# Half of an output product moved into the neighbourhood attention, experts in overlapping pairs, weights laid out in one piece, and value products with odd and even keys abreast

## The chip, the cores and the metric

The kernel runs on one core of one Trainium2 chip, in one launch. Times are device microseconds. The inputs are rearranged on the host before the launch (a function `layout`), which is not timed. All matrices are float32; most products are made of three matmuls on numbers split into a high and a low half.

## The reference, cut to what matters

Two blocks run after each other on 512 tokens of 1024 numbers, each with two layers. A layer of the first block is an attention mixer, a cross attention to a memory, and a mixture of experts in which every expert takes its 64 best tokens. A layer of the second block projects the normed and modulated tokens into four groups of 256 columns (a Fourier mix, neighbourhood attention, a spatial gating and differential attention), joins them in one output product, and adds a feed-forward part. In layer 0 of this block 256 context tokens are carried along.

```python
def expert_choice_moe(h, w_router, w_gate, w_up, w_down):
    ...
    x_in = jax.vmap(lambda hb, ib: hb[ib])(h, idx)
    a = jnp.einsum('becd,edf->becf', x_in, w_gate)
    u = jnp.einsum('becd,edf->becf', x_in, w_up)
    y = jnp.einsum('becf,efd->becd', jax.nn.silu(a) * u, w_down)
    y = y * gate[..., None].astype(y.dtype)
    return jax.vmap(lambda ib, yb: jnp.zeros((S, D), yb.dtype).at[ib.reshape(-1)].add(yb.reshape(-1, D)))(idx, y)

def diff_attend(q1, q2, k1, k2, v, lam):
    scale = DIFF_QK_DIM ** -0.5
    s1 = jnp.einsum('bqhd,bkhd->bhqk', q1, k1).astype(jnp.float32) * scale
    s2 = jnp.einsum('bqhd,bkhd->bhqk', q2, k2).astype(jnp.float32) * scale
    p = jax.nn.softmax(s1, axis=-1) - lam * jax.nn.softmax(s2, axis=-1)
    return jnp.einsum('bhqk,bkhd->bqhd', p.astype(v.dtype), v)

def second_block(x, c, ctx, ...):
    ...
        y = jnp.concatenate([y_a, y_b, y_c, y_d], axis=-1) @ w_out[l]
    ...
        x = x + g1 * y
```

## The kernel before, in words

Tokens lie transposed: a tile `x` holds 128 of the 1024 numbers of all 512 tokens, and eight such tiles the whole state; `cx` are the same for the context. Tiles come from pools with a fixed number of buffers per name (the tables `MIX`, `EXP`, `DIF` and so on; those that begin with `P_` are of PSUM). Each engine works through its own queue in order. A scheduler fixes these orders when the kernel is built, from the order in which the code is written and from modelled times.

A weight comes as a raw tile `wr` from SyncE's DMA queue (L288), is split by ScalarE (L334) into `wh` and by VectorE (L335) into the rest `wl`; `mm3` (L347) then issues three matmuls for each product, at L353, L354 and L356. Activations are split in the same way by `split` (L358).

The experts (`experts`, L872) go in four groups of four. A group gathers its tokens with one-hot matmuls (L888) into `xin`. Then two pairs of experts follow. For each expert of a pair eight steps multiply `xin` with the gate and the up weights (L930; their two results of 64 rows stand in the two halves of a PSUM tile), ScalarE scales the result into `au`, PE transposes it (L936), ScalarE and VectorE make the gated `gg` of it (L938, L939). When both experts of the pair have their `gg`, the second product with the down weights follows (L948, the pair's two experts abreast), is scaled and split into `yy` (L365, L366), and is spread back to the tokens (L956). Weights (`we`) are 1 MB each, two for each of gate, up and down of an expert; their pool has 14 buffers in layer 0 and 12 in layer 1 (`NWE`). On the device a load takes 2 KB in one piece, four pieces for each partition.

In block 2 the stage `nat` (`na`, L1187) goes through units of one head and 128 queries: scores (L1209, L1210), softmax, transposes (L458), and products with the values (L492). The stage `dif` (`diff`, L1256) does so for the differential attention: `stacks` (L1244) copies 32-row pieces of queries and keys by DMA (L1252) into `w`, two score tiles `pD` of up to 768 keys follow (L1292), each with a maximum (L1295) and an exponent (L1296), a combination of both (L1302), transposes (L458), and six value products into one half of a PSUM tile (L492), which ScalarE copies out (L1319). At the end of a half of the heads, `finish` norms and splits the result.

The output product is written as a generator: eight column chunks `c`, in each a sum over eight row chunks `es`, a step being one `mm3`. `fill` (L476) takes steps of it and puts them behind PE's newest instruction. Before, `es` 0 to 5 (48 steps) are filled into `dif`, two steps per unit, and what is left of them, and `es` 6 and 7, follow in the stage `out`. The halves that it multiplies are `YX` and `YC`, made by `parts` (L1505); for the Fourier and gating results this is done at the start of `dif`, in `begin`.

Of the kernel before, what the change touches and what calls it, by code (L numbers as in the profile page):

```python
# [17 lines left out]
D = 1024  # L18
# [121 lines left out]
def layout(a):  # L140
# [18 lines left out]
    for n in ("ln_ffn", "sgu_ln_g_2", "sgu_ln_b_2", "sgu_b_2", "diff_lq1_2", "diff_lk1_2", "diff_lq2_2",  # L159
              "diff_lk2_2", "w_gate", "w_up", "w_down", "ada_w_2"):  # L160
        o[n] = a[n]
    for l in range(2):
# [23 lines left out]
        o[f"w2_out{l}"] = chunks(a["w_out_2"][l][:768], 2)  # L186
        o[f"w2_last{l}"] = chunks(a["w_out_2"][l][768:], 8)
# [12 lines left out]
NWE = (14, 12)  # L200
FIN = 0
NAP = 0
FILL = (2, 0, 0)
# [4 lines left out]
NAB = 7  # L208
# [10 lines left out]
HEADS = {"h": 18, **NORMS}  # L219
MIX = {"f": 4, "e": 3, "pt": 4, "sqm": 3, "lat": 6, "kg": 4, "qk": 12, "kr": 2, "vg": 2, "vm": 1, "wk": 2,  # L220
       "rope1": 1, "rope2": 1, "perm": 1, "wrt": 1}
# [15 lines left out]
P_WIN = {"pS": 4, "pT": 2, "pO": 2}  # L237
# [11 lines left out]
class Kernel:  # L249
# [622 lines left out]
    def experts(k, l, routed):  # L872
        nc = k.nc
        slots, slot, (aH, aL), T = routed
        for g in range(4):
            oh = []
            for t in range(4):
                o = k.t("oh", (128, 4, 64), F32R)
                nc.vector.tensor_tensor(o, slots, slot[:, t, 4 * g:4 * g + 4].unsqueeze(2).to_broadcast([128, 4, 64]),
                                        op=OP.is_equal)  # L880
                oh.append(o.rearrange("p e s -> p (e s)"))
            xin = [k.t("xin", (128, NK, 128)) for _ in range(2)]
            for c in range(NK + 1):
                p = k.ps("mm")
                for t in range(4):
                    for j in range(2):
                        w = T[t][j][:, c * 128:c * 128 + 128] if c < NK else (aH, aL)[j][:, t, :]
                        nc.tensor.matmul(p[:w.shape[1], :256], w, oh[t], start=(t == 0 and j == 0), stop=(t == 3 and j == 1))  # L888
                if c < NK:
                    gain = k.gain(("ln_ffn", l), c)  # L890
                    nc.vector.tensor_scalar(xin[0][:, c], p[:, :128], gain, None, op0=OP.mult)
                    nc.scalar.activation(xin[1][:, c], p[:, 128:256], AF.Copy, scale=gain)
                else:
                    ga = k.t("ga", (17, 256))
                    nc.vector.tensor_copy(ga, p[:17, :256])
            gates, roots, ohT = [], [], []
            for pr in range(2):
                p = k.ps("T")
                nc.tensor.transpose(p[:, :17], ga[:, pr * 128:pr * 128 + 128], k.ident[:17, :17])
                gt = k.t("s1", (128, 1))  # L900
                for h in range(2):
                    a = slice(64 * h, 64 * h + 64)
                    e = 4 * g + 2 * pr + h
                    nc.vector.tensor_copy(gt[a], p[a, e:e + 1])
                    r = k.t("s1", (128, 1))
                    for b in (slice(0, 64), slice(64, 128)):
                        nc.vector.tensor_copy(r[b], p[a, 16:17])
                    roots.append(r)
                gates.append(gt)
                p = k.ps("T")  # L910
                for t in range(4):
                    nc.tensor.transpose(p[:, t * 128:(t + 1) * 128],
                                        oh[t][:, pr * 128:pr * 128 + 128].bitcast(F32), k.ident)
                o = k.t("ohT", dt=F32R)
                nc.scalar.activation(o, p, AF.Copy)
                ohT.append(o)
            for pr in range(2):
                G = []
                for h in range(2):
                    e = 4 * g + 2 * pr + h  # L920
                    s = slice(h * 64, h * 64 + 64)
                    W = {}
                    for n in ("w_gate", "w_up"):
                        for kh in range(2):
                            W[n, kh] = k.load("we", k.i[n][l, e, kh * 512:kh * 512 + 512].rearrange(
                                "(c p) f -> p c f", p=128), (128, 4, 512))
                    p = k.ps("mm")
                    for c in range(NK):
                        for a, n in ((0, "w_gate"), (64, "w_up")):
                            nc.tensor.matmul(p[a:a + 64], xin[pr][:, c, s], W[n, c // 4][:, c % 4],  # L930
                                             start=(c == 0), stop=(c == NK - 1))
                    au = k.t("au")
                    nc.scalar.activation(au, p, AF.Copy, scale=roots[2 * pr + h])
                    p = k.ps("T", (128, 4, 128))
                    for t in range(4):
                        nc.tensor.transpose(p[:, t, :], au[:, t * 128:(t + 1) * 128], k.ident)  # L936
                    gg = k.t("gg", (128, 4, 64))
                    nc.scalar.activation(gg, p[:, :, 0:64], AF.Silu)  # L938
                    nc.vector.tensor_mul(gg, gg, p[:, :, 64:128])  # L939
                    G.append(gg)  # L940
                WD = [[k.load("we", k.i["w_down"][l, 4 * g + 2 * pr + h, :, half * 512:half * 512 + 512].rearrange(
                    "(c p) f -> p c f", p=128), (128, 4, 512)) for h in range(2)] for half in range(2)]
                yH, yL = k.t("yy", (128, D), F32R), k.t("yy", (128, D), F32R)
                for half in range(2):
                    p = k.ps("mm")
                    for t in range(4):
                        for h in range(2):
                            nc.tensor.matmul(p[64 * h:64 * h + 64], G[h][:, t, :], WD[half][h][:, t],  # L948
                                             start=(t == 0), stop=(t == 3))
                    s = slice(half * 512, half * 512 + 512)  # L950
                    k.split(p, yH[:, s], yL[:, s], scale=gates[pr])
# [547 lines left out]
    def groups(k, l, mod, gains, last):  # L1499

        nc = k.nc
        with k.scope(f"proj{l}", PROJ):
# [38 lines left out]
            with k.scope(f"pg{l}", P_DIF, PSUM), k.scope(f"dif{l}", DIF):  # L1541
# [37 lines left out]
                for _ in adds:  # L1579
                    pass  # L1580
# [147 lines left out]
```

## Time and profile before

| | us |
|---|---|
| median of three runs | 3131.39 (3127.49 to 3134.98) |
| the profiled execution | 3128.51 |
| its span in the trace | 3126.7 |
| PE busy | 2971.6 |
| VectorE busy | 1581.2 |
| ScalarE busy | 1205.4 |
| GpSimd busy | 280.7 |

The span is what the trace covers of the profiled execution. PE's time counts each stretch in which at least one matmul is under way. The mean granted clock of PE is 0.97 of its full 2.4 GHz.

### The profile page before, as it was taken

How to read it: one execution, taken by the hardware profiler on the slowest of the kernel's cores; microseconds unless marked ns; L12 is line 12 of the kernel's file. 1: busy time of each engine (PE TensorE's matmuls, PEld its weight loads, DVE VectorE, ACT ScalarE, POOL GpSimd, SP SyncE). 2: the span in 40 equal slices, each digit the busy share in tenths (PEclk: the TensorE clock that was granted, in tenths of full speed). 3: DMA queues.
4: the chain of work that ended last, by engine and by line, in shares of the span. 5: the costliest groups of instructions: out<-in, count | busy, mean ns of one | idle time of the engine just before them, and what ended most of it. 6: DMA issues, size and time to landing. Idle time of an engine off the chain costs nothing.

```text
span 3126.7 us, 42254 instructions
## 1 busy us (share of the span) xinstructions
PE 2971.6 (95%) x16816; PEld 2241.4 (72%) x16816; DVE 1581.2 (51%) x3071; ACT 1205.4 (39%) x2356; POOL 280.7 (9%) x281
## 2 busy tenths in 40 slices
PE   8999979998999988999998899999999998999998
PEld 5677764444666864444887778888888787878887
DVE  5666652224576644234537666334344547654444
ACT  4646431113565532113426554222222336542332
POOL 2111120001102101001300011000000100010000
PEclk9999989999999998999999899999999998999999
DMA  5423249994433228996222311111111222222221
GB/s 183 135 95 122 95 180 332 358 370 172 161 109 115 82 78 316 367 370 242 62 74 70 90 41 55 68 55 68 68 54 54 97 96 71 65 81 95 94 98 64
DMA packets 168756, 422.34 MB, mean 135 GB/s; under 512 B 12144, under 2 KB 21616, under 8 KB 152816
## 3 DMA queue, kind: packets, MB, share of 16 engines
q1 hardware_dynamic: 167536, 416.76, 37.9%
q0 software_dynamic: 1024, 2.89, 0.4%
q8 instruction: 133, 2.18, 0.3%
q14 instruction: 63, 0.52, 0.0%
HBM read 405.18 MB, written 2.10 MB: 130 GB/s over the span
## 4 chain that ended last, share of the span: by engine, by line
PE 89%; DVE 4%; ACT 3%; issue 1%; DMA 1%; POOL 0%; SPq 0%; POOLq 0%; ACTq 0%; DVEq 0%
PE pmm L354 12%; PE pmm L353 12%; PE pmm L356 12%; PE pmm L930 8%; PE pS L353 5%; PE pS L356 4%; PE pS L354 4%; PE pmm L948 4%; PE pT L458 4%; PE pO L704 3%; PE pmm L888 2%; PE pA L998 2%; PE pmm L956 2%; PE pT L492 2%; PE pT L394 1%
## 5 line engine op out<-in xcount | busy, mean ns | idle before, releaser
L334 ACT ACTIVATE wh<-wr 128x1024 fp32r<-128x1024 f32 (+1 forms) x195 | 202.3, 1038 | 533.7 <-PE pmm L354 364.9
L335 DVE TENSOR_TENSOR wl<-wr,wh 128x1024 fp32r<-128x1024 f32 (+1 forms) x195 | 242.0, 1244 | 279.4 <-ACT wh L334 279.0
L930 PE MATMUL pmm<-we,xin 128*64 128x512 f32 x1024 | 238.1, 596 | 0.0
L353 PE MATMUL pS<-h,wh 128*128 128x512 f32 (+1 forms) x480 | 190.0, 400 | 12.5 <-ACT wh L334 10.2
L1616 DVE SCALAR_TENSOR_TENSOR x<-pmm,ada,x 128x512 f32<-128x512 f32 (+1 forms) x136 | 95.5, 717 | 206.4 <-PE pmm L356 206.3
L354 PE MATMUL pmm<-h,wh 128*128 128x512 f32 (+1 forms) x480 | 186.1, 389 | 2.7 <-DVE h L1036 2.6
L354 PE MATMUL pS<-h,wh 128*128 128x512 f32 (+1 forms) x480 | 185.2, 386 | 3.3 <-DVE h L366 3.3
L356 PE MATMUL pS<-h,wl 128*128 128x512 f32 (+1 forms) x480 | 185.2, 390 | 1.9 <-DVE wl L335 1.9
L356 PE MATMUL pmm<-h,wl 128*128 128x512 f32 (+1 forms) x480 | 184.0, 385 | 0.0
L353 PE MATMUL pmm<-h,wh 128*128 128x512 f32 (+1 forms) x480 | 182.9, 390 | 0.9 <-ACT h L1031 0.9
L334 ACT ACTIVATE vh<-wr 128x1024 fp32r<-128x1024 f32 x68 | 71.8, 1060 | 272.9 <-PE pmm L354 237.3
L930 PEld LDWEIGHTS pmm<-we,xin 128*64 128x64 f32 x1024 | 72.8, 137 | 136.8 <-issue 128.8
L379 POOL TENSOR_TENSOR sq<-sq,sq 128x512 f32<-128x512 f32 (+1 forms) x49 | 61.0, 1245 | 1174.7 <-ACT sq L371 1137.6
L948 PE MATMUL pmm<-we,gg 128*64 128x512 f32 x512 | 143.1, 605 | 15.1 <-DVE gg L939 15.1
L460 ACT ACTIVATE pt<-pT 128x512 f32<-128x512 f32 (+1 forms) x200 | 109.6, 554 | 118.9 <-PE pT L458 118.4
L335 DVE TENSOR_TENSOR vl<-wr,vh 128x1024 fp32r<-128x1024 f32 x68 | 83.7, 1233 | 114.0 <-ACT vh L334 114.0
L353 PE MATMUL pmm<-hid,vh 128*128 128x512 f32 (+1 forms) x400 | 139.3, 348 | 0.0
L439 DVE TENSOR_REDUCE s<-pS 128x1 f32<-128x512 f32 (+1 forms) x200 | 124.2, 622 | 27.8 <-PE pS L356 22.0
L354 PE MATMUL pmm<-hid,wh 128*128 128x512 f32 (+1 forms) x400 | 133.9, 350 | 0.0
L354 PE MATMUL pmm<-hid,vh 128*128 128x512 f32 (+1 forms) x400 | 133.8, 347 | 0.0
L353 PE MATMUL pmm<-hid,wh 128*128 128x512 f32 (+1 forms) x400 | 131.3, 349 | 0.0
L446 ACT ACTIVATE e<-pS,s,rt 128x512 f32<-128x512 f32 (+1 forms) x160 | 117.4, 734 | 17.6 <-DVE s L441 17.2
(443 smaller groups left out, 7179.0 us busy)
## 6 DMA issues: line engine op xcount, KB each, us to landing
we<-in_w_gate_dram SPq DMA_DIRECT2D x64, 1024.0 KB, 11.1
we<-in_w_up_dram SPq DMA_DIRECT2D x64, 1024.0 KB, 10.6
we<-in_w_down_dram SPq DMA_DIRECT2D x64, 1024.0 KB, 13.5
wr<-in_w_ff_dram SPq DMA_DIRECT2D x64, 1024.0 KB, 4.8
wra<-in_ada_w_dram SPq DMA_DIRECT2D x96, 512.0 KB, 4.2
wr<-in_w_in_dram SPq DMA_DIRECT2D x27, 1024.0 KB, 4.8
wr<-in_w_o_dram SPq DMA_DIRECT2D x8, 1024.0 KB, 4.8
wr<-in_w_mkv_dram SPq DMA_DIRECT2D x8, 1024.0 KB, 4.9
```

The lines of the kernel that those rows point to most:

```text
L334: k.nc.scalar.activation(H[:, :m], raw[:, a:a + m], AF.Copy)
L335: k.nc.vector.tensor_sub(L[:, :m], raw[:, a:a + m], H[:, :m].bitcast(F32))
L353: mm(p, wH, xH, start=(first and j == 0), stop=False)
L354: mm(p, wH, xL, start=False, stop=False)
L356: mm(p, wL, xH, start=False, stop=(end and j == n - 1))
L439: nc.vector.reduce_max(m, s, axis=AX, negate=True)
L446: nc.scalar.activation(e, s, AF.Exp, bias=m, scale=1.0 if scale is None else scale, accum_out=z)
L458: k.nc.tensor.transpose(p[:, t - a, :], src[:, t * 128:(t + 1) * 128], k.ident)
L460: k.nc.scalar.activation(dst[:, a:b], p[:, :b - a, :], AF.Copy)
L930: nc.tensor.matmul(p[a:a + 64], xin[pr][:, c, s], W[n, c // 4][:, c % 4], start=(c == 0), stop=(c == NK - 1))
L948: nc.tensor.matmul(p[64 * h:64 * h + 64], G[h][:, t, :], WD[half][h][:, t], start=(t == 0), stop=(t == 3))
L1616: nc.vector.scalar_tensor_tensor(x, p, mod[:, 40 + o, j:j + 1], x, op0=OP.mult, op1=OP.add)
```

## The change

In the experts, `gather` holds what was at the head of a group, `opened` the first products of a pair up to `gg`, and `closed` its second product and the spreading. `closed` of a pair is written behind `opened` of the next. The gate, up and down weights, and those of `ada`, are laid out so that a partition's share of a load is one piece (8 KB, and 4 KB for `ada`). Pools get other sizes, and the weights' pool of the mixer another place. In `nat` the units go head by head, each head's operands are made when its turn comes, and 32 steps of the output product (part 0, `es` 0, 1, 4, 5) are spread over the units by a due count. The parts that these need are made at the start of `nat`, with the subtraction on GpSimd. In `dif` part 1 (`es` 2, 3; 16 steps) is filled, one step per unit, and `out` has part 2. `halved` takes the place of `weigh` for the differential values: even keys go to the lower half of the PSUM tile, odd keys to the upper, ScalarE copies one half and VectorE adds the other.

```diff
-NWE = (14, 12)
+NWE = (13, 11)
-FILL = (2, 0, 0)
+FILL = (1, 0, 0)
...
-ROUTED = {"ht": 8, "ap": 2, "slots": 1, "oh": 4, "ga": 1, "xin": 2}
+ROUTED = {"ht": 8, "ap": 2, "slots": 1, "oh": 4, "ga": 1, "xin": 3}
 MOE = {"e16": 5, "m8": 2, "raw": 3}
-EXP = {"au": 2, "gg": 3, "yy": 3, "ohT": 2}
+EXP = {"au": 2, "gg": 4, "yy": 3, "ohT": 3}
...
-P_WIN = {"pS": 4, "pT": 2, "pO": 2}
+P_WIN = {"pS": 3, "pT": 2, "pO": 1, "pD": 1}
...
+    for n in ("w_gate", "w_up"):
+        o[n] = np.ascontiguousarray(a[n].reshape(2, 16, 2, 4, 128, 512).transpose(0, 1, 2, 4, 3, 5))
+    o["w_down"] = np.ascontiguousarray(a["w_down"].reshape(2, 16, 4, 128, 2, 512).transpose(0, 1, 4, 3, 2, 5))
...
+    def halved(k, e, v, nt, o, tag, work=None):
+
+        pt, p = k.t(tag, (128, nt, 128)), None
+        k.transposed(e, nt, pt, work=work)
+        p = k.ps("T", (128, 128))
+        for t in range(nt):
+            k.nc.tensor.matmul(p[64 * (t % 2):64 * (t % 2) + 64], v(t), pt[:, t, :], start=(t < 2), stop=(t >= nt - 2))
+        k.nc.scalar.activation(o, p[64:], AF.Copy)
+        k.nc.vector.tensor_add(o, o, p[:64])
...
     def experts(k, l, routed):
...
+        left = None
         for g in range(4):
...
+            for pr, (xin, gate, roots, ohT) in enumerate(k.gather(l, g, routed)):
+                G = k.opened(l, 2 * g + pr, xin, roots)
+                if left is not None:
+                    k.closed(l, *left)
+                left = 2 * g + pr, G, gate, ohT
+        k.closed(l, *left)
...
-        nc.vector.tensor_sub(low[other], src[rows], dst[rows].bitcast(F32))
...
+        nc.gpsimd.tensor_copy(low[other], low[rows].bitcast(F32))
...
-        units = [(j, lo, qc, h) for j in range(2) for lo, nq in ranges for qc in range(nq) for h in range(2)]
...
+        units = [(g, lo, qc) for g in range(4) for lo, nq in ranges for qc in range(nq)]
...
+            due = steps * max(0, n + 1 - 1) // (len(units) - 1)
+            k.fill(other, due - done[0])
+            done[0] = due
...
     def halves(k, y, n):
         parts = [k.t("w", (128, S + C), F32R) for _ in range(2)]
-        k.split(y[:, :n], parts[0][:, :n], parts[1][:, :n])
+        k.nc.scalar.activation(parts[0][:, :n], y[:, :n], AF.Copy)
+        k.nc.gpsimd.tensor_sub(parts[1][:, :n], y[:, :n], parts[0][:, :n].bitcast(F32))
...
+                es, m = (((0, 1, 4, 5), 4), ((2, 3), 8), ((6, 7), 8))[part]
...
             with vals, k.scope(f"pd{l}", P_WIN, PSUM):
-                k.na(l, P, na, V["nv"], bias, not last, lambda j, lo, n, o: parts(2 + j, lo, n, o))
+                for c in (4, 5, 0, 1):
+                    parts(c, 0, S, Y[c][:, :S], nc.gpsimd)
+                    if not last:
+                        parts(c, S, C, Y[c][:, S:], nc.gpsimd)
+                work = adds(0)
+                k.na(l, P, na, V["nv"], bias, not last, lambda j, lo, n, o: parts(2 + j, lo, n, o), work, 4 * NK)
+                for _ in work:
+                    pass
...
-                k.scope(f"wa{l}", WTS2, side="right"), k.scope(f"heads{l}", HEADS), k.scope(f"mix{l}", MIX):
+                k.scope(f"wa{l}", WTS2), k.scope(f"heads{l}", HEADS), k.scope(f"mix{l}", MIX), k.scope(f"mixo{l}", MIXO):
```

The order of PE in layer 0's experts, first pair to second product; `gg` 4608 and 4643 before, 4617 and 4652 after, belong to the first pair's two experts. Before:

```order
L930 MATMUL pmm_4619<-we_4613,xin_4439 64x512
L930 MATMUL pmm_4619<-we_4617,xin_4439 64x512
L930 MATMUL pmm_4619<-we_4613,xin_4439 64x512
L930 MATMUL pmm_4619<-we_4617,xin_4439 64x512
L948 MATMUL pmm_4656<-we_4646,gg_4608 64x512
L948 MATMUL pmm_4667<-we_4650,gg_4608 64x512
L936 MATMUL pT_4638<-c_ident,au_4636 128x128 x4
L948 MATMUL pmm_4656<-we_4648,gg_4643 64x512
L948 MATMUL pmm_4656<-we_4646,gg_4608 64x512
```

After, lines 945, 951 and 967 are what 930, 936 and 948 were:

```order
L945 MATMUL pmm_4698<-we_4692,xin_4449 64x512
L945 MATMUL pmm_4698<-we_4696,xin_4449 64x512
L951 MATMUL pT_4682<-c_ident,au_4680 128x128 x4
L945 MATMUL pmm_4698<-we_4692,xin_4449 64x512
L945 MATMUL pmm_4698<-we_4696,xin_4449 64x512
L967 MATMUL pmm_4735<-we_4725,gg_4617 64x512
L967 MATMUL pmm_4735<-we_4727,gg_4652 64x512
L967 MATMUL pmm_4735<-we_4725,gg_4617 64x512
L967 MATMUL pmm_4735<-we_4727,gg_4652 64x512
```

Before, the second product begins on the first expert's `gg` alone, with the partner's transposes still to come. After, first products of the next pair (`pmm_4698`) and its transposes stand ahead, and both `gg` are used from the first row on.

The order of PE at the start of layer 0's neighbourhood attention, from the second unit on. Before:

```order
L1209 MATMUL pS_14231<-na_13952,na_13949 128x256
L1210 MATMUL pS_14231<-na_13953,na_13949 128x256
L1209 MATMUL pS_14231<-nc_13970,na_13949 128x256
L1210 MATMUL pS_14231<-nc_13971,na_13949 128x256
L1209 MATMUL pS_14257<-na_13943,na_13940 128x256
L1210 MATMUL pS_14257<-na_13944,na_13940 128x256
L1209 MATMUL pS_14257<-nc_13961,na_13940 128x256
L1210 MATMUL pS_14257<-nc_13962,na_13940 128x256
L1209 MATMUL pS_14282<-na_13952,na_13949 128x256
L1210 MATMUL pS_14282<-na_13953,na_13949 128x256
```

After (1234 and 1235 are the scores, 361, 362 and 364 the three matmuls of `mm3`):

```order
L1234 MATMUL pS_14240<-na_13956,na_13953 128x256
L1235 MATMUL pS_14240<-na_13957,na_13953 128x256
L1234 MATMUL pS_14240<-nc_13965,na_13953 128x256
L1235 MATMUL pS_14240<-nc_13966,na_13953 128x256
L361 MATMUL pD_14256<-h_14216,wh_14248 128x512
L362 MATMUL pD_14256<-h_14217,wh_14248 128x512
L361 MATMUL pD_14256<-hc_14220,wh_14248 128x256
L1234 MATMUL pS_14283<-na_13956,na_13953 128x256
L1235 MATMUL pS_14283<-na_13957,na_13953 128x256
L1234 MATMUL pS_14283<-nc_13965,na_13953 128x256
L1235 MATMUL pS_14283<-nc_13966,na_13953 128x256
L362 MATMUL pD_14256<-hc_14221,wh_14248 128x256
```

Before, scores follow on scores. After, the first step of the output product, on the parts `h_14216` and `hc_14220`, stands behind the second unit, and the other scores behind it.

The order of ScalarE between the last expert of layer 0 and the mixer of layer 1. Before:

```order
L365 ACTIVATE yy_6027<-pmm_6029,s_1464_5799 128x512
L365 ACTIVATE yy_6027<-pmm_6040,s_1464_5799 128x512
L365 ACTIVATE h_6111<-x_58,c_gains 128x512
L371 ACTIVATE sq_6115<-x_58 128x512
L371 ACTIVATE sq_6121<-x_59 128x512
L371 ACTIVATE sq_6127<-x_60 128x512
L371 ACTIVATE sq_6134<-x_61 128x512
L365 ACTIVATE h_6117<-x_59,c_gains 128x512
L334 ACTIVATE wh_6168<-wr_6166 128x1024
L334 ACTIVATE wh_6172<-wr_6166 128x1024
```

After (373 scales and norms, 342 splits the weight, 379 squares):

```order
L373 ACTIVATE yy_6036<-pmm_6038,s_1449_5744 128x512
L342 ACTIVATE wh_6180<-wr_6178 128x1024
L342 ACTIVATE wh_6184<-wr_6178 128x1024
L373 ACTIVATE yy_6036<-pmm_6049,s_1449_5744 128x512
L1017 ACTIVATE condz_9957<-cond_9955 128x8x2
L373 ACTIVATE h_6123<-x_58,c_gains 128x512
L379 ACTIVATE sq_6127<-x_58 128x512
```

The split of the mixer's first weight stood behind the last scaling, two norms' products and four squares; now it stands between the last two scalings.

## Rows read from the trace of the kernel before

**Rows 1.** The page, part 1: busy us, share of the span, instructions
```profile
PE 2971.6 (95%) x16816; PEld 2241.4 (72%) x16816; DVE 1581.2 (51%) x3071; ACT 1205.4 (39%) x2356; POOL 280.7 (9%) x281
```

**Rows 2.** The page, costliest groups: busy, mean ns | idle before
```profile
L930 PE MATMUL pmm<-we,xin 128*64 128x512 f32 x1024 | 238.1, 596 | 0.0
L948 PE MATMUL pmm<-we,gg 128*64 128x512 f32 x512 | 143.1, 605 | 15.1 <-DVE gg L939 15.1
```

**Rows 3.** Waits of PE: total us, times, longest us
```profile
PE pmm L948 <- DVE gg L939: 15.1, 16, 1.0
PE pS L1209 <- ACT h L446: 11.7, 4, 6.9
```

**Rows 4.** Windows of block 2's attention stages, columns as the first line
```profile
core 0: us, PE busy (x) PEld busy (x) DVE busy (x) ACT busy (x) POOL busy (x), PEclk, DMA share, GB/s
1669.00:1726.00 57.00, 45.78 (x325) 37.48 (x323) 41.74 (x112) 32.33 (x84) 1.70 (x3) 0.91 0.18 49
1726.00:1742.00 16.00, 9.21 (x32) 7.70 (x32) 11.22 (x20) 7.41 (x18) 2.96 (x6) 0.58 0.50 126
1742.00:1852.00 110.00, 106.43 (x722) 89.23 (x720) 73.18 (x147) 63.81 (x161) 6.52 (x9) 1.00 0.21 56
2587.00:2628.00 41.00, 36.11 (x256) 31.16 (x255) 28.70 (x74) 22.85 (x52) 0.50 (x1) 0.92 0.16 49
2628.00:2642.00 14.00, 7.95 (x30) 6.39 (x28) 10.25 (x17) 8.78 (x18) 2.48 (x5) 0.68 0.54 122
2642.00:2713.00 71.00, 68.30 (x469) 56.87 (x469) 53.09 (x88) 46.44 (x108) 5.61 (x9) 0.99 0.24 64
```

**Rows 5.** Windows of the experts, last a feed-forward weight's load; same columns
```profile
463.00:742.00 279.00, 268.92 (x1288) 127.31 (x1288) 79.79 (x193) 47.27 (x93) 0.31 (x1) 0.99 0.91 331
500.00:560.00 60.00, 59.07 (x292) 28.62 (x291) 19.25 (x47) 9.19 (x19) 0.00 (x0) 1.00 0.99 362
560.00:640.00 80.00, 77.22 (x366) 35.40 (x363) 22.13 (x52) 13.39 (x26) 0.00 (x0) 1.00 1.01 371
2012.00:2013.50 1.50, 1.50 (x10) 1.27 (x10) 1.05 (x2) 0.00 (x0) 0.00 (x0) 1.00 1.00 426
```

**Rows 6.** Timeline at the mixer of layer 1: start, duration, instruction [idle before]
```profile
744.30 0.51 PE L353 MATMUL pS<-h,wh 128*128 128x512 f32 x1 [2.14 <-ACT wh L334]
...
747.12 0.79 PE L356 MATMUL pS<-h,wl 128*128 128x512 f32 x1 [1.91 <-DVE wl L335]
```

**Rows 7.** Timeline of PE in layer 0's differential stage, one filler step
```profile
1797.89 0.40 PE L353 MATMUL pD<-h,wh 128*128 128x512 f32 x1
1798.13 0.40 PE L354 MATMUL pD<-h,wh 128*128 128x512 f32 x1
...
1798.94 0.39 PE L353 MATMUL pD<-h,wh 128*128 128x512 f32 x1
```

**Rows 8.** The page, costliest groups: GpSimd
```profile
L379 POOL TENSOR_TENSOR sq<-sq,sq 128x512 f32<-128x512 f32 (+1 forms) x49 | 61.0, 1245 | 1174.7 <-ACT sq L371 1137.6
```

**Rows 9.** Timelines at the entry of the differential stage: SyncE's queue, PE
```profile
1726.77 15.78 SPq L1252 DMA_DIRECT2D w<-w  x18
...
1731.48 2.26 PE L1292 MATMUL pD<-w,w 128*128 128x256 f32 x9 [5.39 <-DMA w<-w]
```

**Rows 10.** Groups by line, whole span: value products and ScalarE's copy
```profile
L492 PE MATMUL pT<-pt,dv 128*64 128x128 f32 x416 | 54.5, 278 | 4.2 <-ACT pt L460 4.1
...
L704 PE MATMUL pO<-pt,vm 128*64 128x128 f32 x512 | 45.3, 283 | 0.0
...
L1319 ACT ACTIVATE f<-pT 64x128 f32<-64x128 f32 x40 | 10.7, 269 | 13.7 <-PE pT L492 13.4
```

**Rows 11.** Groups of VectorE in the differential stage, layer 0
```profile
L1295 DVE TENSOR_REDUCE s<-pD 128x1 f32<-128x768 f32 x28 | 25.7, 952 | 18.2 <-PE pD L1292 18.2
...
L1568 DVE SCALAR_TENSOR_TENSOR x<-pD,ada,x 128x512 f32<-128x512 f32 x7 | 5.2, 750 | 4.4 <-PE pD L356 4.4
...
L1568 DVE SCALAR_TENSOR_TENSOR cx<-pD,ada,cx 128x256 f32<-128x256 f32 x7 | 3.3, 475 | 0.0
```

More of the change, by code (lines that the diff above doesn't have):

```diff
@@ L207 @@
 LAG = 2
-NAB = 7
 OFF = 2
@@ L870, in route, with gather @@
         return slots, slot, (aH, aL), T
-    def experts(k, l, routed):
+    def gather(k, l, g, routed):
         nc = k.nc
         slots, slot, (aH, aL), T = routed
-        for g in range(4):
[L876 to L951, printed above, removed]
-                for cols in (HALVES if l and g == 3 and pr == 1 else (ALL,)):
-                    for c in range(NK):
-                        p = k.ps("mm")[:, cols]
-                        for y in (yH, yL):
-                            nc.tensor.matmul(p, y[:, c * 128:c * 128 + 128], ohT[pr][:, cols], start=(y is yH), stop=(y is yL))
-                        nc.vector.tensor_add(k.x[c][:, cols], k.x[c][:, cols], p)
@@ new lines, in closed @@
+    def closed(k, l, n, G, gate, ohT):
+        nc = k.nc
+        WD = [[k.load("we", k.i["w_down"][l, 2 * n + h, half], (128, 4, 512)) for h in range(2)] for half in range(2)]
+        yH, yL = k.t("yy", (128, D), F32R), k.t("yy", (128, D), F32R)
+        for half in range(2):
+            p = k.ps("mm")
+            for t in range(4):
+                for h in range(2):
+                    nc.tensor.matmul(p[64 * h:64 * h + 64], G[h][:, t, :], WD[half][h][:, t], start=(t == 0), stop=(t == 3))
+            s = slice(half * 512, half * 512 + 512)
+            k.split(p, yH[:, s], yL[:, s], scale=gate)
+        for cols in (HALVES if l and n == 7 else (ALL,)):
+            for c in range(NK):
+                p = k.ps("mm")[:, cols]
+                for y in (yH, yL):
+                    nc.tensor.matmul(p, y[:, c * 128:c * 128 + 128], ohT[:, cols], start=(y is yH), stop=(y is yL))
+                nc.vector.tensor_add(k.x[c][:, cols], k.x[c][:, cols], p)
@@ L1449, in projections @@
         values_.enter_context(k.scope(f"nat{l}", NAT))
-        na = {0: k.na_prepare(P["nq", 0], P["nk", 0], not last, ("na", "nc"))}
+        na = {h: k.na_prepare(P["nq", 0], P["nk", 0], h, not last) for h in range(2)}
         bias = {h: k.bias(l, h) for h in range(2)}
@@ new lines, in adds @@
+            def adds(part):
+                for c in range(NK):
+                    yield from add(c, part, both)
+            both = ((0, ALL),) if last else ((0, ALL), (1, CTX))
+            with vals, k.scope(f"pd{l}", P_WIN, PSUM):
+                for c in (4, 5, 0, 1):
[6 more added lines that the diff above has]
+                    pass
@@ L1572, in both_adds @@
-                def both_adds():
-                    for c in range(NK):
-                        yield from add(c, True, both)
-                both = ((0, ALL),) if last else ((0, ALL), (1, CTX))
-                adds = both_adds()
-                k.diff(l, P, halves, dv, nlam, not last, begin, lambda j, lo, n, y: parts(6 + j, lo, n, y), adds)
+                dv = [V["dv"][128 * t] for t in range(4)] + [V["dv"]["c", t] for t in range(2)]
+                work = adds(1)
+                k.diff(l, P, halves, dv, nlam, not last, lambda j, lo, n, y: parts(6 + j, lo, n, y), work)
@@ L1578, in groups @@
                 mark(k, f"out{l}")
-                for _ in adds:
+                for _ in work:
                     pass
-                w[1] = k.weights(k.i[f"w2_last{l}"][0])
                 k.F = [k.pairs("h", S)] if last else [k.pairs("h", S), k.pairs("hc", C)]
@@ L1676, in run @@
     ctx = k.ctx
+    ctx.enter_context(k.scope("edge", {"edge": 1}, side="right"))
+    k.nc.gpsimd.memset(k.t("edge", (128, 24)), 0.0)
     ctx.enter_context(k.scope("small", SMALL))
```

198 lines of the change are left out of this document (126 added, 72 removed).

## The prediction

> **What bounds the kernel now.** I read the profile page first. TensorE (PE) is busy 95% of the span [rows 1], so a change pays in two ways only: it takes work from PE, or closes one of the gaps in its 155 us of idle time (3126.7 - 2971.6). Then the table by line: the experts' two products are among the costliest groups, and the second one, L948, is worse per pass than the first, though both write 512 columns from 64 rows with two results abreast: 143.1/512 = 0.279 us against 238.1/1024 = 0.233 us [rows 2]. The waits of PE name the reason: 16 times it stands for the gated activations `gg`, about 0.94 us each [rows 3]. Then windows by stage in block 2, whose attention stages leave PE most idle: in layer 0, 11.2 of 57 us in the neighbourhood attention, 6.8 of 16 at the entry to the differential attention, but only 3.6 of 110 in its body, where VectorE is at 73 of 110 [rows 4]. The body is where the output product stands as filler now; the neighbourhood attention has none.
>
> **Experts.** There are 16 pairs (two layers of eight). Passes of one pair at the price of L930 would make L948 119.1 us; it takes 143.1, so 24.0 are lost because its first passes run alone while the partner's `gg` is late, and 15.1 more are waits [rows 2, 3]: 39.1/16 = 2.45 us per pair. In the new order the next pair's first products stand between, so that both `gg` exist long before they are read. The last pair of each layer has no successor, so 14 gain: 34 us at most. I take **-31**, since the transposes between products still cost switches, with 22 to 36 as ends.
>
> This holds only if the weights come fast enough. A pair takes 12 loads of 1024 KB, 12.58 MB, eight pairs 100.7 MB. With 2 KB pieces the 16 DMA engines are already full in the middle of the stage, at a share of 0.99 to 1.01 and 362 to 371 GB/s [rows 5]; 100.7 MB at that rate takes 271 to 278 us, and the whole stage lasts 279. So the pipelined order alone would find the DMA at its limit and win 1 to 8 us a layer, 2 to 16 in all. The new layout gives each partition 8 KB in one piece. The feed-forward weights already have such pieces, and inside one such load the engines moved 426 GB/s at a share of 1.00 [rows 5]. At 426 the 100.7 MB take 236 us, under the 279 - 15.5 = 263 that PE would then need. I take the layout as the condition of the gain, at zero by itself: PE hides it. The smaller ring (13 and 11 slots for 14 and 12) still holds nearly a pair's loads.
>
> A rule speaks against this: the Trainium skill, DMA: Bandwidth & Descriptors, "Where 436 GB/s comes from", says that for loads from device memory the memory side, about 358 GB/s per core, binds and not the fabric's 435. By it a pair would need 35 us, and the experts would gain nothing. The trace does not agree as far as it goes: 371 GB/s over 80 us, and 426 over 1.5 us in a single load [rows 5]; no row shows 390 or more for long. It has its chance as a rival below.
>
> **Mixer of layer 1.** The split weights' pool moves to the side where it no longer waits for the experts' last tiles, and in the new order of ScalarE its two casts stand ahead of the last scaling (2 us by them, under the spreading of the first half). At its start PE waits 2.14 us for `wh` and 1.91 for `wl` [rows 6]. Both are 4.05; **-4** (2 if another input is late there next, the norm's factors say, and 6 if the passes behind the two waits speed up too).
>
> **The groups of block 2.** The output product is 64 steps of three-matmul sums a layer. Of 48 that stood in the differential stage, 32 now stand in the neighbourhood attention and 16 stay. A step is six matmuls; start to start in layer 0 it takes 1798.94 - 1797.89 = 1.05 us [rows 7]. Layer 1 has no context columns, so only the three 512-column ones: 3 x 0.233 = 0.70 us.
>
> Neighbourhood, layer 0: 32 x 1.05 = 33.6 us come in. They can use the 11.2 idle us [rows 4]. But the first step stands third on PE, and its operands are copies that start only when the projections' tiles come free, each with a subtraction on GpSimd; the nearest row, a 128x512 one, takes 1.25 us [rows 8]. Four of these are 5 us, about 4 of which PE will stand, in the place of the 6.9 us it waits there now for the first softmax [rows 3]. So 33.6 - 11.2 + 4 = **+26** (20 to 32). Layer 1: 22.4 - 4.9 + 1 = **+18** (14 to 24).
>
> Entry to the differential stage: PE stands 5.39 us for the gathered `w` tiles, whose 18 DMAs are issued late [rows 9], because they sit behind the release of the tiles that the copies above read. Those copies are now done a stage earlier, the stacks can be built under the neighbourhood's end, and 16 us become about 3.5 (one step and the first nine scores): **-12.5**, and **-10** of 14 in layer 1.
>
> Body, layer 0: PE loses 28 of the 44 steps in this window, 29.4 us, and the values' products get cheaper: with odd and even keys in the two column halves the nearest rows, L704, run at 45.3/512 = 0.088 us a pass against 54.5/416 = 0.131 [rows 10]: 0.043 x 224 passes here = 9.6. PE then has 106.4 - 39 = 67 us of work. VectorE has 73.2 plus one addition per unit from PSUM; no row shows a 64x128 one there; ScalarE's copy of that shape is 0.27 us [rows 10], the reduction over 768 columns 0.95 [rows 11]. Between nothing (if it fell wholly into waits) and the 0.475 of 256 columns [rows 11], that is 0 to 11 us for 24 units, I take 0.27, the same shape: 6.5. 80 us of VectorE, and a tenth for its waits: 89. So **-21** (-10 if it stays as loosely packed as today, -28 if it packs fully). Layer 1: 53.1 + 16 x 0.27 = 57.4, with 5% of waits 60 of 71: **-11** (-5 to -14).
>
> Tail: the chain that ends the last head (norm, gain, split) was covered by 24 leftover matmuls of the product, now by 9: 15 matmuls, 2.6 us, and more at the low clock: **+4.5** (3 to 7) and **+3** in layer 1.
>
> Layer 0 sums to 26 - 12.5 - 21 + 4.5 = -3, layer 1 to 18 - 10 - 11 + 3 = 0. Groups: **-3** (-25 to +20 with the ends above). The subtractions moved from VectorE to GpSimd I price at nothing: GpSimd is busy 1.7 of 57 us there [rows 4]; without that room each costs the unit that reads it 1.25 us [rows 8].
>
> **Sum.** -31 - 4 - 3 = -38, on the profiled execution's 3128.5: 3090.5. The median of the runs shown is 2.9 us above that execution, so the forecast for the median is **3093**.
>
> **Rivals.**
> (a) The experts stay bound by the DMA: 8 KB pieces hold no more than the 371 GB/s of the sustained row [rows 5]. Then 2 to 16 us there, say 9, in place of 31: 3115. For it: no long stretch above 371. Against: the 426 inside one load.
> (b) The differential stage doesn't speed up, since its chain (scores, maximum, exponent, combination, transposes, products) sets the pace and not PE. VectorE waits 18.2 us there for the scores of L1292 [rows 11], which speaks against. Then the neighbourhood's +44 gets back only the 22.5 at the entries and 5: groups +24 in place of -3: 3120.
> (c) The body is set by PE alone and packs tightly: 110 to 80 and 71 to 55 with a nearly full neighbourhood (+20, +14): groups -24, 3072.
> (d) Slower than before: in the neighbourhood attention the filler's result has one PSUM buffer (`pD`), and PE goes in order. Every eighth of the product ends with VectorE adding it to `x` and `cx`, 0.75 + 0.475 us [rows 11], behind whatever softmax stands in its queue, and the next eighth's first matmul, and all scores behind it, wait. At 14 such places, it takes 3.1 us each (44/14, up to 3137) to make the kernel slower. The bare additions are 1.2 us, and other products of PE stand between in most places, so it would need a queue of 2 us of softmax every time.
> (e) That the entry gains nothing, as the stacks' copies still sit late in the DMA queue: +22, 3115.
>
> **Chances.** Forecast (3078 to 3108) 0.52; (a) 0.12; (b) 0.12; (c) 0.12; (d) 0.06; (e) 0.06. A change within 0.2%, 6 us, can't be told from none for this kernel. (a) and (e) are faster still, (b) mostly. Faster 0.87, same 0.07, slower 0.06. The range 3064 to 3120 takes in (a), (c), (e) and leaves out (d) and part of (b).
>
> **What would show it.** Right: the second expert product near 0.233 us a pass with no wait for `gg`; DMA near 390 GB/s in the experts and its share under 1; neighbourhood windows of about 83 and 59 us, entries under 5, bodies about 89 and 60. Wrong: waits of PE for `we`; VectorE idle and waiting for PE in the body; PE waiting for `x` additions ahead of `pD`.

## The result, and the profile after

The changed kernel takes 3084.41 us (median of four, 3084.09 to 3095.92) beside 3131.01 of the kernel before: a ratio of 0.986, interval 0.9834 to 0.9885. 3093 was forecast, with a range of 3064 to 3120. A control run of the same kernel on another occasion gave 3088.79 (3084.01 to 3096.18), ratio 0.9885 (0.9868 to 0.9903). Of the eight executions five lie between 3084.0 and 3085.4 and three between 3092 and 3096. The profiled one of the first four is a late one: 3095.92, span 3094.1; that of the control ran 3084.01, span 3082.2. Six of the 12 us between them are there before the experts' first matmul (461.9 us after the start against 455.9). In the first 104 us the clock that TensorE (PE) was granted was lower, 0.93 of its full clock in the first and 0.98 in the second of these windows (the columns are those of [rows 4]):

```profile
0.00:104.00 104.00, 91.96 (x431) 67.67 (x432) 53.96 (x93) 51.27 (x81) 24.59 (x23) 0.93 0.48 170
```

```profile
0.00:104.00 104.00, 91.87 (x450) 67.45 (x450) 57.01 (x103) 53.04 (x83) 25.60 (x24) 0.98 0.51 179
```

So pieces of a few us are read below with this spread in mind, and the experiments by their medians.

In the experts, these groups answer to [rows 2]:

```profile
L945 PE MATMUL pmm<-we,xin 128*64 128x512 f32 x1024 | 239.5, 596 | 0.0
...
L967 PE MATMUL pmm<-we,gg 128*64 128x512 f32 x512 | 134.0, 597 | 0.0
```

The second product no longer waits for `gg`: its idle time, 15.1 us before, is nothing. But its busy time is 134.0 us, where the price of the first product makes 119.8; only 9 of the 24 us that passes lost by running alone, without the partner expert's beside them, have gone. And one of PE's waits has grown (total us, times, longest us), from 2 to 12 waits of about 0.78 us for the split results `yy` ahead of the spreading (L956 before, L974 now). Before and after:

```profile
PE pmm L956 <- ACT yy L365: 1.6, 2, 0.8
...
PE pmm L974 <- ACT yy L373: 9.3, 12, 0.8
```

The windows of block 2's attention stages, which answer to [rows 4] in the same order (the neighbourhood attention, then the entry and the body of the differential stage; layer 0, then layer 1):

```profile
1646.40:1732.50 86.10, 78.58 (x514) 67.07 (x512) 57.75 (x126) 41.27 (x96) 18.83 (x23) 0.96 0.32 86
1732.50:1736.00 3.50, 2.21 (x14) 1.60 (x12) 2.93 (x4) 1.99 (x4) 0.00 (x0) 1.00 0.08 33
1736.00:1829.10 93.10, 79.37 (x578) 58.73 (x577) 78.79 (x177) 64.34 (x166) 6.37 (x9) 0.95 0.16 42
2559.40:2617.80 58.40, 55.95 (x354) 45.51 (x352) 43.09 (x90) 32.05 (x65) 7.22 (x10) 1.00 0.34 103
2617.80:2622.00 4.20, 2.42 (x13) 1.90 (x12) 3.28 (x4) 2.46 (x6) 0.00 (x0) 0.89 0.00 0
2622.00:2688.70 66.70, 55.87 (x440) 41.81 (x439) 57.68 (x109) 49.04 (x112) 5.13 (x8) 0.96 0.16 36
```

The neighbourhood grew from 57 to 86 us and from 41 to 58; the entries shrank from 16 and 14 to 3.5 and 4.2; the bodies from 110 and 71 to 93.1 and 66.7. VectorE is now busy for 78.8 of 93.1 us in the first body, PE for 79.4: neither is full.

By stage, first to last matmul, the span of 3126.7 became 3094.1 thus: experts 279.0 to 268.4 and 284.8 to 276.7 (-18.7); the attention stages with the output product and the start of the feed-forward part, -1.1 and -1.7; the rest -11.1, of which -3.9 in the feed-forward stage of layer 0 with the next projections and -3.3 in that of layer 1, stages in which the change edits nothing.

### The profile page after: what moved, and what is told of

It is laid out like the page before. It is cut to its first block, busy times and chain, and to the rows that moved or that the text cites. A ratio compares the mean times of both kernels' runs of the same rounds, so it can differ in the third digit from the quotient of the medians.

```text
span 3094.1 us, 42320 instructions
## 1 busy us (share of the span) xinstructions
PE 2934.6 (95%) x16816; PEld 2211.6 (71%) x16816; DVE 1590.4 (51%) x3095; ACT 1205.7 (39%) x2352; POOL 323.1 (10%) x318
## 4 chain that ended last, share of the span: by engine, by line
PE 86%; DVE 7%; ACT 4%; issue 1%; DMA 1%; POOL 1%; SPq 0%; POOLq 0%; DVEq 0%; ACTq 0%
PE pmm L361 12%; PE pmm L362 12%; PE pmm L364 12%; PE pmm L945 8%; PE pS L361 5%; PE pS L362 4%; PE pS L364 4%; PE pmm L967 4%; PE pT L466 3%; PE pO L722 3%; PE pmm L906 2%; PE pmm L974 2%; PE pA L1026 2%; PE pT L402 1%; PE pD L361 1%
## 5 line engine op out<-in xcount | busy, mean ns | idle before, releaser
L967 PE MATMUL pmm<-we,gg 128*64 128x512 f32 x512 | 134.0, 597 | 0.0
```

## The experiments

All are the changed kernel with one edit, except "before, with the pad", which is the kernel before with one, and the last, which has two. Each was timed beside the kernel before, whose medians were 3127.0, 3127.7 and 3128.3 on three occasions (the first four rows of the table, the next four, the last four).

| run | median us | ratio to before, interval |
|---|---|---|
| control | 3088.79 | 0.9885 (0.9868 to 0.9903) |
| spreading last | 3070.11 | 0.9812 (0.9796 to 0.9827) |
| pairs in turn | 3106.07 | 0.9932 (0.9920 to 0.9945) |
| small pieces | 3085.29 | 0.9869 (0.9855 to 0.9882) |
| filler back | 3084.09 | 0.9869 (0.9845 to 0.9892) |
| one half | 3093.49 | 0.9891 (0.9873 to 0.9909) |
| pool back | 3087.56 | 0.9878 (0.9858 to 0.9898) |
| no pad | 3099.30 | 0.9911 (0.9895 to 0.9927) |
| before, with the pad | 3114.85 | 0.9961 (0.9946 to 0.9976) |
| pad of 64 bytes | 3097.00 | 0.9904 (0.9888 to 0.9919) |
| pad of 192 bytes | 3100.64 | 0.9913 (0.9896 to 0.9929) |
| spreading last, filler back | 3065.81 | 0.9801 (0.9785 to 0.9817) |

**The control.** The kernel as it is.

> The changed kernel itself, as a control for the other runs on this chip. Three of its four executions so far lay at 3084 us, the profiled one at 3096. Theory: the typical time is 3084 and the trace shows one execution that lost 11 us somewhere. Rival: the kernel has a wide spread of its own and the median of more runs lies near 3090.

Neither quite: 3084 is the most frequent time, and a quarter to a half of the executions are 8 to 12 us later. A difference under some 5 us between two medians says nothing.

**Spreading last.** The order of PE that the changed kernel was built with has two kinds of pairs. In 6 of 16 the second product's rows stand together, as shown ahead of the prediction. In the other 10, the later ones of each layer, the spreading of the first half (L974) stands between the two halves of the second product (L967).

The timeline of PE in the changed kernel shows such a pair, and what the order costs (start, duration, instruction, idle time before):

```profile
635.37 0.66 PE L951 MATMUL pT<-c_ident,au 128*128 128x128 f32 x4 [0.82 <-ACT au L948]
635.95 3.65 PE L967 MATMUL pmm<-we,gg 128*64 128x512 f32 x16
640.38 2.21 PE L974 MATMUL pmm<-ohT,yy 128*128 128x512 f32 x8 [0.77 <-ACT yy L373]
642.51 3.65 PE L967 MATMUL pmm<-we,gg 128*64 128x512 f32 x14
646.94 2.14 PE L974 MATMUL pmm<-ohT,yy 128*128 128x512 f32 x8 [0.78 <-ACT yy L373]
```

There are three waits in 12 us: for `au`, since transposes of the next pair come between the passes, and twice for `yy`, which ScalarE has only just begun to scale. This is one of the three worst pairs; six others wait once for `yy`, and one does not. The edit lets the spreading be issued only behind the last pass of the second half:

```diff
-        for cols in (HALVES if l and n == 7 else (ALL,)):
...
+        pe = nc.tensor.engine
+        with k.tc.issue_after(next(i for i in reversed(nc.cur_bb.bb.instructions) if i.engine == pe)):
+            for cols in (HALVES if l and n == 7 else (ALL,)):
...
```

> In the experts the spreading back to the tokens may only be issued after both halves of the second product. Theory: in 10 of 16 pairs the new order puts the spreading of the first half between the halves, where TensorE waits twice 0.78 us for the split result and passes run alone; without that the experts gain 12 to 20 us more: 3064 to 3072. Rival: the DMA sets the pace of the experts (0.96 to 0.98 of its time in the middle of the stage), so the waits only come back as waits for weights: 3080 to 3086.

3070.11, 18.7 less than the control and 14.3 less than the first median. In its trace the second product takes 125.9 us, 8 less, and the waits for the scaled half are gone (9.3 us), while those for `x` ahead of the spreading grow from 2.0 to 4.1 us. From the first expert pass to the last spreading the two stages take 252.2 and 256.2 us for 257.2 and 266.2, 15.0 less. The rival's waits for weights did not come.

```profile
L967 PE MATMUL pmm<-we,gg 128*64 128x512 f32 x512 | 125.9, 595 | 0.0
```

**Pairs in turn.** Each pair's second product stands right behind its own first one again.

```diff
-                if left is not None:
-                    k.closed(l, *left)
-                left = 2 * g + pr, G, gate, ohT
-        k.closed(l, *left)
+                k.closed(l, 2 * g + pr, G, gate, ohT)
```

> The changed kernel with each pair's second products written right behind its own first ones again; layout, pools and everything else as changed. Theory: the overlap of the pairs is worth what the experts' stages got shorter by, 10.6 and 8.1 us: 3100 to 3106. Rival: the layout alone made them shorter, by faster loads: 3084 to 3088.

3106.07, 17 to 22 us more than the changed kernel. The wait for `gg` and most of the passes that run alone are back, and the two stages take 267.5 and 274.1 us, as before the change (267.6 and 274.3):

```profile
L967 PE MATMUL pmm<-we,gg 128*64 128x512 f32 x512 | 141.8, 598 | 13.9 <-DVE gg L954 13.9
```

**Small pieces.** The gate, up and down weights as in the kernel before, 2 KB in one piece; their loads' lines as before.

```diff
-    for n in ("w_gate", "w_up"):
-        o[n] = np.ascontiguousarray(a[n].reshape(2, 16, 2, 4, 128, 512).transpose(0, 1, 2, 4, 3, 5))
...
-            W = {(name, kh): k.load("we", k.i[name][l, 2 * n + h, kh], (128, 4, 512))
+            W = {(name, kh): k.load("we", k.i[name][l, 2 * n + h, kh * 512:kh * 512 + 512].rearrange("(c p) f -> p c f", p=128), (128, 4, 512))
```

> The changed kernel with the experts' weights in pieces of 2 KB again. Theory: 100.7 MB a layer in 268 to 276 us is 365 to 376 GB/s, right at what these pieces gave before (362 to 371), so the stage gets 4 to 10 us longer a layer and TensorE waits for weights: 3092 to 3104. Rival: the layout does nothing for the time, since the loads are hidden in either form: 3083 to 3087.

The rival was right: 3085.29, no difference. The windows of this run's experts (last columns: clock, share of the DMA engines, GB/s):

```profile
490.00:560.00 70.00, 70.00 (x352) 32.41 (x350) 20.84 (x50) 12.03 (x24) 0.00 (x0) 1.00 1.05 387
560.00:640.00 80.00, 78.40 (x384) 35.69 (x382) 24.34 (x56) 13.10 (x26) 0.00 (x0) 1.00 1.05 387
```

The same windows of the changed kernel:

```profile
490.00:560.00 70.00, 70.00 (x354) 32.34 (x352) 20.84 (x50) 12.03 (x24) 0.00 (x0) 1.00 0.98 405
560.00:640.00 80.00, 78.77 (x388) 35.15 (x384) 21.26 (x51) 13.47 (x27) 0.00 (x0) 1.00 0.96 395
```

Small pieces keep the engines busier (1.05 for 0.98) but move 387 GB/s, not 371. PE has no wait for `we` in either trace. So the 362 to 371 of [rows 5], at a share of 0.99 to 1.01, was what PE asked for, not what the engines could do. Small pieces together with the faster order of "Spreading last" were not tried.

**Filler back.** All 48 steps in the differential stage, two per unit; nothing in the neighbourhood attention.

```diff
-FILL = (1, 0, 0)
+FILL = (2, 0, 0)
...
-                work = adds(0)
-                k.na(l, P, na, V["nv"], bias, not last, lambda j, lo, n, o: parts(2 + j, lo, n, o), work, 4 * NK)
-                for _ in work:
-                    pass
+                k.na(l, P, na, V["nv"], bias, not last, lambda j, lo, n, o: parts(2 + j, lo, n, o), iter(()), 4 * NK)
...
-                work = adds(1)
+                work = chain(adds(0), adds(1))
```

> The changed kernel with no filler in the neighbourhood attention: all 48 steps stand in the differential stage again, two per unit; the parts made early and the values abreast stay. The changed kernel is at 3084 to 3089. Theory: moving the filler is about neutral in the changed kernel (28 and 17 us more in one stage, 30 and 13 less in the next), and what it brings is the freed entry, which stays here; the body then is bound by TensorE at 96 us in layer 0, the neighbourhood back at 58: 3066 to 3080. Rival: filler in the neighbourhood fills idle time that nothing else fills, and without it each layer loses 8 to 15 us: 3100 to 3115.

3084.09, between the two ranges: neither came true, and the move is neutral, as the theory's first sentence had it, but without the gain that its range stood for. The windows of layer 0 (neighbourhood, entry, body):

```profile
1649.30:1712.90 63.60, 48.38 (x321) 39.40 (x320) 44.58 (x106) 36.62 (x92) 18.96 (x23) 0.89 0.34 85
1712.90:1720.00 7.10, 4.49 (x20) 3.29 (x20) 6.33 (x12) 4.98 (x13) 0.00 (x0) 0.88 0.01 3
1720.00:1829.60 109.60, 100.58 (x731) 78.98 (x730) 86.86 (x183) 64.30 (x159) 6.14 (x9) 0.99 0.17 45
```

180.3 us in all, against 182.7 in the changed kernel's. What the neighbourhood loses without the filler (22.5 us), the entry and the body take back (3.6 and 16.5 more): PE is then busy 100.6 of 109.6 us in the body, and VectorE, with its additions, 86.9. From the end of the body to the feed-forward part's first product with its hidden tiles `hid` it takes 74.2 us, in the changed kernel 70.6.

**One half.** The differential values' products as in the kernel before (`weigh` for `halved`).

```diff
-            k.halved(e, lambda t: v[t0 + t][:, (2 * j + h) * 64:(2 * j + h) * 64 + 64], 6 - t0, o[j, lo][rows, cols], "pt6", work)
+            p = k.weigh(e, lambda t: v[t0 + t][:, (2 * j + h) * 64:(2 * j + h) * 64 + 64], 6 - t0,
+                        lambda: k.ps("T", (128, 128))[rows], "pt6", 6, work)
+            nc.scalar.activation(o[j, lo][rows, cols], p, AF.Copy)
```

> The changed kernel with the differential values' products in one half of the PSUM tile, one after the other, as before; no addition on VectorE. Theory: TensorE is idle for 13.7 of 93 us in the body of layer 0, so the cheaper products are partly lost to waits: 2 to 8 us slower, 3088 to 3095. Rival 1: the 18 us that TensorE saves in the two layers all count: 3100 to 3106. Rival 2: VectorE sets the pace and is rid of 40 additions: 3076 to 3083.

3093.49, inside the theory's range: 5 to 9 us more than the two medians of the changed kernel. The intervals overlap, so that the loss is likely but not clear of the spread. PE's passes take 54.9 us here:

```profile
L500 PE MATMUL pT<-pt,dv 128*64 128x128 f32 x416 | 54.9, 278 | 6.0 <-ACT pt L468 5.8
```

and 33.9 in the changed kernel, where VectorE's additions take 11.1:

```profile
L509 PE MATMUL pT<-pt,dv 128*64 128x128 f32 x416 | 33.9, 289 | 7.5 <-ACT pt L468 7.4
...
L511 DVE TENSOR_TENSOR f<-f,pT 64x128 f32<-64x128 f32 x40 | 11.1, 278 | 11.9 <-ACT f L510 11.4
```

So of the 21 us that PE saves, some 5 to 9 reach the time, going by the medians.

**Pool back.** The mixer's weight pool on its old side.

```diff
-                k.scope(f"wa{l}", WTS2), k.scope(f"heads{l}", HEADS), k.scope(f"mix{l}", MIX), k.scope(f"mixo{l}", MIXO):
+                k.scope(f"wa{l}", WTS2, side="right"), k.scope(f"heads{l}", HEADS), k.scope(f"mix{l}", MIX), k.scope(f"mixo{l}", MIXO):
```

> The changed kernel with the mixer's weight pool on its old side, so that the first split waits again for the experts' last tiles. Theory: the stretch from the experts of layer 0 to those of layer 1 got 2.3 us shorter, and that comes back: 3086 to 3091. Rival: the place of the pool also changes addresses, on which the rate of the matmuls may hang, and more than 5 us come back: 3092 to 3100.

3087.56, not to be told from the changed kernel. The waits did come back, and larger (timeline of PE at the mixer of layer 1):

```profile
728.92 0.80 PE L361 MATMUL pS<-h,wh 128*128 128x512 f32 x1 [4.72 <-ACT wh L342]
...
730.84 0.79 PE L364 MATMUL pS<-h,wl 128*128 128x512 f32 x1 [0.70 <-DVE wl L343]
```

But the changed kernel waits there too, for the norm's products `h`:

```profile
726.74 0.50 PE L362 MATMUL pS<-h,wh 128*128 128x512 f32 x1 [1.35 <-DVE h L374]
...
729.09 0.50 PE L362 MATMUL pS<-h,wh 128*128 128x512 f32 x1 [0.21 <-DVE h L374]
...
732.33 0.50 PE L362 MATMUL pS<-h,wh 128*128 128x512 f32 x1 [1.56 <-DVE h L374]
```

These are 3.12 us in all, for 4.05 before the change [rows 6]. What the rival named, the address, is in the trace too: with the pool on its old side the mixers' passes take longer, here one of their three lines, pool back and control:

```profile
L364 PE MATMUL pS<-h,wl 128*128 128x512 f32 (+1 forms) x480 | 186.1, 392 | 0.7 <-DVE wl L343 0.7
```

```profile
L364 PE MATMUL pS<-h,wl 128*128 128x512 f32 (+1 forms) x480 | 183.7, 387 | 0.0
```

Where passes of 512 columns follow each other without a gap they start 232.5 ns apart on average with the pool back, 228.1 in the control and 233.3 in the kernel before. By an estimate from these starts that is 5 us over the two layers, which the medians neither show nor exclude; the edit also changes PE's order in some places.

**No pad.** The change has one more line: `run` also makes a tile of 24 numbers (96 bytes) at the right end of the memory, which nothing reads.

```diff
-    ctx.enter_context(k.scope("edge", {"edge": 1}, side="right"))
-    k.nc.gpsimd.memset(k.t("edge", (128, 24)), 0.0)
```

> The changed kernel without the pad of 24 numbers at the right end of the memory and its memset. Theory: the matmuls of 512 columns start 227.8 ns apart in the last feed-forward stage where it was 230.2, and the two feed-forward stages got 4 to 5 us shorter though nothing in them changed; the pad shifts the addresses of the pools on that side, and without it the rate falls back: 8 to 16 us slower, 3092 to 3102. Rival: the addresses moved by other pools' sizes, or the rate is another one in every execution: 3082 to 3088.

3099.30: the theory's range. The pad is worth 10 to 15 us. Its trace in a stretch of the last feed-forward stage, 280 us at the full clock with PE busy throughout (second column in brackets: matmuls), without the pad and in the control:

```profile
2773.00:3053.00 280.00, 280.00 (x1218) 228.46 (x1217) 128.90 (x151) 82.72 (x103) 0.00 (x0) 1.00 0.27 94
```

```profile
2760.00:3040.00 280.00, 280.00 (x1231) 230.78 (x1230) 129.59 (x152) 83.94 (x104) 0.00 (x0) 1.00 0.26 94
```

The order of PE's instructions is the same in both. The kernel before, in the same stretch of the program:

```profile
2800.00:3080.00 280.00, 280.00 (x1219) 228.41 (x1218) 128.72 (x151) 82.59 (x102) 0.00 (x0) 1.00 0.26 94
```

The traces also tell which operand it is. In the second block the only tiles that lie on the right beside the pad are the split weights `wh` and `wl`; the feed-forward part's other weights, `vh` and `vl`, come from a pool on the left. Both are multiplied with the same `hid`. Without the pad, then in the control (busy us, mean ns of one):

```profile
L362 PE MATMUL pmm<-hid,wh 128*128 128x512 f32 (+1 forms) x400 | 133.9, 350 | 0.0
L362 PE MATMUL pmm<-hid,vh 128*128 128x512 f32 (+1 forms) x400 | 133.8, 347 | 0.0
```

```profile
L362 PE MATMUL pmm<-hid,vh 128*128 128x512 f32 (+1 forms) x400 | 133.8, 347 | 0.0
L362 PE MATMUL pmm<-hid,wh 128*128 128x512 f32 (+1 forms) x400 | 132.9, 347 | 0.0
```

Only the passes with `wh` change. From start to start, those of 512 columns with `wh` and `wl` are 232.9 ns apart without the pad and 229.5 with it; those with `vh` and `vl` are 229.7 apart in both.

**The pad alone, in the kernel before.**

> The kernel before with nothing but the pad of 24 numbers and its memset added. Theory: the pad shifts the split weights of the second block by 96 bytes and with that sets the rate of the matmuls whatever else is changed: 10 to 16 us faster, 3111 to 3118 beside 3127. Rival: the pad is worth something only with the new sizes of the pools, which moved the other tiles too: 3124 to 3130.

3114.85, 13.4 us less than before with no other change, and the same count of matmuls as in the control:

```profile
2790.00:3070.00 280.00, 280.00 (x1231) 230.78 (x1230) 129.57 (x152) 83.92 (x104) 0.00 (x0) 1.00 0.26 94
```

**Pads of other sizes.** `(128, 16)` and `(128, 48)` in place of `(128, 24)`; the order of PE's instructions is the same.

> The changed kernel with a pad of 16 numbers (64 bytes for 96). The changed kernel is at 3084 to 3089, without a pad at 3099. Theory: the rate depends on where a row starts within 64 bytes, so a shift by 64 is as none: 3096 to 3101. Rival: any shift that takes the rows from the old places will do: 3082 to 3090.

> The changed kernel with a pad of 48 numbers (192 bytes for 96). Theory (within 64 bytes): 192 is again as none, 3096 to 3101. Rival (any shift will do): 3082 to 3090.

3097.00 and 3100.64: both as without a pad, and so are the counts.

```profile
2773.00:3053.00 280.00, 280.00 (x1218) 228.24 (x1217) 128.59 (x151) 82.51 (x102) 0.00 (x0) 1.00 0.26 94
```

```profile
2778.00:3058.00 280.00, 280.00 (x1216) 228.30 (x1215) 128.57 (x151) 82.55 (x102) 0.00 (x0) 1.00 0.26 94
```

**Spreading last and filler back.**

> The changed kernel with the spreading behind both halves and with the filler back in the differential stage. Theory: the two are in different stages and add: spreading -16 to -19, filler 0 to -4: 3062 to 3071. Rival: the filler in the neighbourhood only breaks even because other waits end later, and without the waits of the experts nothing changes for it: 3070 to 3075.

3065.81, the lowest median of all, and clear of the changed kernel; against spreading last alone (3070.11) it is within the spread. So the moved filler is worth nothing that can be seen here either.

## Why the prediction was right, point by point

The time came out 9 us under the forecast, and the direction for the reason given first, the experts. But the experts' and the mixer's terms were too large, and one term was missing. That the total came so close is luck: the experts brought some 13 us less than their term, and the pad, which has no term, brought 10 to 15.

**Experts, -31: the size was off.** The mechanism was right: the wait for `gg` is gone, and taking the overlap back costs 17 to 22 us, 18.2 of them in the two stages; the lower end of the term was 22. The term gave 14 pairs the full 2.2 us. It was read off the first pairs' order, and 10 of 16 pairs have another, which puts waits for `yy` in place of those for `gg`. With that mended the gain is 3106.07 - 3070.11 = 36.0 us by the medians and 33.2 in the two stages, near the 34 that 14 pairs at 2.45 us gave at most.

**The layout as the condition: wrong.** The step took the rate of a stage whose pace PE sets for the most that 2 KB pieces can carry. They carried 387 GB/s when PE asked for more. Rival (a) fell with it. So did the rival by the memory's limit: the Trainium skill, DMA: Bandwidth & Descriptors, "Where 436 GB/s comes from", has about 358 GB/s per core, half of what two cores share, as what binds such loads. The trace does not agree: the changed kernel, on its one core, moved 405 GB/s over 70 us, well past it, and the measurement decides.

**Mixer, -4: nothing to be seen in the time.** The lower end's reason held: another input, the norm's products, is late there next, and 4.05 us of waits became 3.12. That the place of the pool also changes the spacing of the mixers' passes was not in the term.

**Groups, -3.** The stages of both layers, up to the feed-forward part's first product with `hid`, came out at -2.8 in the trace. In the trace without the pad they take 252.1 and 192.2 us, for 254.4 and 192.0 before the change: some -2. So the sum held, but by terms that were off both ways: the neighbourhood +29 and +17 (forecast +26 and +18), the entries -12.5 and -9.8 (-12.5 and -10), the bodies -17 and -4 (-21 and -11), the tails to that product -0.7 and -5.2 (+4.5 and +3; without the pad +0.2 and -3.9). Why the tails did not grow was not tested. The ends that the prediction names add up to about +28 for the groups, not to the +20 that it states. The stall for GpSimd's copies at the neighbourhood's start is there, 2.5 us for `hc` and 1.0 for `h` (forecast 4):

```profile
PE pD L362 <- POOL hc L1538: 2.5, 1, 2.5
...
PE pD L362 <- POOL h L1538: 1.0, 1, 1.0
```

VectorE's addition takes 0.278 us (0.27 assumed) and a pass of the values 33.9/416 = 0.081 (0.088). What was mis-sized is the packing: a tenth of waits was allowed in the body of layer 0 and 5% in layer 1, but VectorE stands idle for 15% and 14%. Rival (b), a body set by its chain, is half true: in that of layer 1, PE has 55.9 and VectorE 57.7 of 66.7 us. The prediction has no term for the filler's move by itself: its -3 takes in the freed entry and the cheaper value products. The runs show it to be worth nothing.

**The pad: a term that was missing.** It was in the change and not in the sum. By removal from the changed kernel it is worth 10 to 15 us, added to the kernel before 13.4.

**The other rivals** did not come: (c) would have had bodies of 80 and 55 us, for 93.1 and 66.7; for (d), no wait ahead of `pD` for the additions to `x` is over 1.3 us in the traces of the two stages; and for (e), the entries did shrink to 3.5 and 4.2 us.

Put together from the experiments: pad 10 to 15, overlap 17 to 22, values abreast 5 to 9, the rest about nothing: 32 to 46, and 38 to 47 were measured. The parts made early, with GpSimd's subtractions, and the new sizes of the pools had no run of their own.

## What to carry to other kernels

An order that is fixed by a scheduler has to be read to its end: the first pairs of a loop showed the intended overlap, and most of the later ones did not. A rate read from a stage in which another engine sets the pace is what was asked for, and no limit. A line of a change that computes nothing (a pad) can be worth as much as its largest part; where stages that nobody edited get faster, compare the spacing of their instructions first.

## What the runs showed of the hardware that was not expected

Shifting the tiles at the right end of the memory by 96 bytes changes the rate of three-matmul products in the feed-forward stage: 1231 for 1219 matmuls in 280 us at the full clock, 227.5 for 229.7 ns each, 1%. 64 and 192 bytes do nothing (1218 and 1216). It is the place of the split weights `wh` and `wl` that matters there: their passes start 232.9 ns apart without the pad, 232.8 and 233.0 with the two other sizes and 229.5 with 96 bytes, while those with `vh` and `vl`, which did not move, stay at 229.6 to 229.7. In the mixers the spacing fell from 233.3 to 228.1 ns when their weights went to the other side.

The three sizes fit a dependence on the start within 64 bytes, which 96 alone of them changes, but they do not prove it. No second size with that remainder, and no other remainder, was tried. The mixers of the kernel before speak against it as the whole rule: their weights lie on the right too, and the same 96 bytes brought them only from 233.3 to 232.5 ns.

The 16 DMA engines moved 405 GB/s over 70 us with pieces of 8 KB and 387 with pieces of 2 KB.
